# A second attention whose columns and row blocks stand between its transposes, scores and values

## The chip, the cores and the metric

One NeuronCore of a Trainium2 chip runs the whole program. The metric is the device time of one execution in microseconds (us); a kernel has several timed runs, and their median counts. Beside them stands one profiled execution, from which every row below comes. Engines are named as in the profile: PE is TensorE's matmuls, PEld its weight loads, DVE is VectorE, ACT is ScalarE, POOL is GpSimd, SP is the engine that issues the weight DMAs.

## What is computed

Two layers of an encoder over 256 rows of width 1024, in fp32. A layer is a half-weighted FFN, an attention, and another half-weighted FFN, each between two RMS norms:

```python
for i in range(DEPTH):
    g = norm_g[i]
    h = h + FFN_RES * _rmsnorm(_swiglu(_rmsnorm(h, g[0]), ffn1_wg[i], ffn1_wu[i], ffn1_wd[i]), g[1])
    u = _rmsnorm(h, g[2])
    if kind == 0:   m = _diff_attention(u, diff_w_in[j], diff_w_out[j], ...)
    elif kind == 1: m = _neighborhood_attention(u, na_w_in[j], na_w_out[j], na_rpb[j])
    h = h + _rmsnorm(m, g[3])
    h = h + FFN_RES * _rmsnorm(_swiglu(_rmsnorm(h, g[4]), ffn2_wg[i], ffn2_wu[i], ffn2_wd[i]), g[5])
```

The first attention is differential: 8 heads with two key halves of 64 each, two softmaxes of which the second is subtracted with a factor. The second one is a neighbourhood attention: 16 heads of 64, where a row sees a band of 16 columns in all four rows of the grid, with a learned bias.

## The kernel before, in words

All products are made with split operands: a weight or an activation x is written as hi + lo (ACT copies hi, DVE subtracts to get lo), and a product is hi*hi + hi*lo + lo*hi. So each 512 KB piece of weights is loaded by SP (L109), copied by ACT (L134), subtracted by DVE (L135), and then used by TensorE. `Weights.get` asks for splits four pieces ahead and for loads up to eight ahead; four raw buffers and nine split buffers are cycled, and a split buffer is free once both row blocks have used its piece.

There are 256 rows, in two blocks of 128. `proj_rows` makes a 128 x 512 block of one row block (24 products, L402); `proj_cols` makes 256 columns, transposed, for all rows (48 products, L428 to L430); `proj_col` does so for 128 columns of an FFN (16 products, L444 and L446) and leaves two half results, which `gu_cols` adds up: ACT copies one out of the bank (L530), DVE adds the other (L531). `row_steps` makes the down and output products (L469). Banks of TensorE's output memory come in three pools: two for projections ("mm"), four for scores, values and sums ("acc"), two for transposes ("tr").

The second attention (`attn` with key "a1") works on two groups g of eight heads. Of each group there are queries and keys as columns (`qk_cols`, one call for four pairs of heads, in two halves c of 256 columns each; only the first group's queries are made as rows, `qk_rows`, and then transposed, `qk_T`), values as rows (`v_rows`, per row block t). A score step `scores(g, qh, pr)` takes query block qh and four heads pr: 24 short products, biased maxima (L689), exponentials (L698), scalings (L713). The scores of pr = 0 need only the first half of the key columns. `probs_T` transposes the result (L378) and splits it; `av_cols(g, pr)` multiplies with the values (L750) once both query blocks are there, and its result is split into `oT`; `wout` multiplies pieces of `oT` with the output weights, into the sums y0 and y1 of the two row blocks. `queue_bias(1)` queues the loads and the writing of the second group's bias table; they are issued one by one behind weight loads, and `W.extra` issues what is left of them.

The order of the code is a priority, not the order of execution: a planner goes through the program in its own times and gives each engine, among the instructions that it holds to be ready, the one that stands first in the code. `tc.high_priority(offset=n)` counts an instruction as n places earlier; HP2 is 100, and `split_bank` (L362) has it already. Each engine then runs its list in that order, and waits where an operand is late. `hooks` of `proj_rows` call a function behind a given product of a block; what it issues on TensorE may then not come earlier.

Of the kernel before, what the change touches and what calls it, by code (L numbers as in the profile page):

```python
# [155 lines left out]
def encoder_kernel(ctx, tc, x, norm_g, f1g, f1u, f1d, f2g, f2u, f2d,  # L156
# [77 lines left out]
    def bank(pool, tag):  # L234
        return pool.tile([P, 512], F32, tag=tag, name=nm(tag))
# [266 lines left out]
    def ffn(key, li, gains, xg1, xT, last, aside=None):  # L502
# [20 lines left out]
        def gu_cols(p):  # L523
            keys = [[(key, n, p * PW, j) for j in range(KT * PW // UE)] for n in "gu"]
            g = t2p.tile([P, 2, S], F32, tag="t2", name=nm("g"))
            u = t2p.tile([P, 2, S], F32, tag="t2", name=nm("u"))
            for k, y in zip(keys, (g, u)):
                for f in range(2):
                    ps = proj_col(xT, k, f)
                    nc.scalar.activation(y[:, f], ps[:, S:], AF.Copy)  # L530
                    nc.vector.tensor_tensor(out=y[:, f], in0=ps[:, :S], in1=y[:, f], op=ALU.add)  # L531
                if y is g:
                    s = act(flat(g))
            a = gated(flat(u), s)
            ht = l4p.tile([P, 2, 2, S], F32R, tag="l4", name=nm("hT"))
            split_bank(flat(ht[:, 0]), flat(ht[:, 1]), a)
            for f in range(2):
                hT[2 * p + f] = (ht[:, 0, f, :], ht[:, 1, f, :])
# [45 lines left out]
    def attn(key, li, gains, xg1, xT):  # L584
# [8 lines left out]
        def v_rows(g, t):  # L593
            ps = mm_tile()
            proj_rows(ps, xT, t, keys_of(2, g))
# [48 lines left out]
        def qk_cols(part, g):  # L644
            qk_tiles(part, g)
            hi, lo = qk[part, g]
            for c in range(2):
# [164 lines left out]
        else:  # L812
            qk_cols(1, 0)
            qk_T(0, 0, 1)
        if diff:
# [11 lines left out]
        if diff:  # L827
# [8 lines left out]
            probs_T(0, 0, 1)  # L836
            o = av(0, 0)
            qk_rows(1, 1, 0)
# [5 lines left out]
            probs_T(0, 1, 1)  # L844
            o = av(0, 1)
            qk_T(1, 1, 1)
# [31 lines left out]
        W.extra(len(W.extras))  # L878
        scores(0, 0, 0)
        scores(0, 1, 0)  # L880
        qk_cols(0, 1)
# [3 lines left out]
        probs_T(0, 0, 0)  # L885
        probs_T(0, 1, 0)
        qk_cols(1, 1)
        av_cols(0, 0)
        probs_T(0, 0, 1)
        probs_T(0, 1, 1)  # L890
# [4 lines left out]
        v_rows(1, 0)  # L895
        scores(1, 0, 1)
        scores(1, 1, 1)
        gpre, gpost = gains()
        v_rows(1, 1)
        y0 = [mm_tile() for _ in range(2)]  # L900
        probs_T(1, 0, 0)
        probs_T(1, 1, 0)
        wout(y0, 0, [0, 1, 2, 3])
        av_cols(1, 0)
        probs_T(1, 0, 1)
        probs_T(1, 1, 1)
        wout(y0, 0, [4, 5])
        av_cols(1, 1)
        y1 = [bank(ps_acc, "acc") for _ in range(2)]
        wout(y1, 1, [0, 1])  # L910
# [83 lines left out]
```

## Time and profile before

| | us |
|---|---|
| median of 3 runs (1009.20 to 1011.17) | 1010.07 |
| profiled execution, its own time | 1012.26 |
| its span, first to last instruction | 1010.0 |
| TensorE matmul busy | 991.0 |
| DVE busy | 676.2 |
| ACT busy | 588.1 |

The stages lie in the span as follows: first FFN to 201, first attention to 320, then two FFNs to 692, second attention to 818, last FFN. A row of the time-ordered view gives start and length in us, then engine, line, operation, output and inputs by the program's names, shapes, a count, and in square brackets the idle time of the engine before it with what ended that. A matmul row is longer than the time from its start to the next start, since matmuls overlap; pace is read from the starts.

### The profile page before, as it was taken

The page shows a single profiled execution, that of the slowest core. Times are in us where ns is not written, and L with a number is a line of the kernel's source. Part 1 is how long each engine was busy: PE and PEld are TensorE (multiplying, and loading weights), DVE is VectorE, ACT ScalarE, POOL GpSimd, SP SyncE. Part 2 cuts the span into 40 slices and gives each one's busy share as a digit, 9 for nine tenths or more (in the row PEclk, how much of TensorE's full clock was granted, in tenths as well). Part 3 has the DMA queues.
Part 4 walks back from the last instruction along what each step waited for, and adds up shares of the span by engine and source line. Part 5 has one row for each costly group of instructions (what it writes and reads, how often), then busy time and mean ns, then how long its engine had stood idle before and what let it go on. Part 6 is the DMA issues. An engine that isn't in the chain of part 4 may idle for free.

```text
span 1010.0 us, 14628 instructions
## 1 busy us (share of the span) xinstructions
PE 991.0 (98%) x5299; PEld 839.2 (83%) x5299; DVE 676.2 (67%) x1282; ACT 588.1 (58%) x1247; POOL 20.7 (2%) x35
## 2 busy tenths in 40 slices
PE   8999999999999999999999999999999999999997
PEld 4888888888777888888888888888898888888886
DVE  6665656577777656566577576658788687556562
ACT  6655555466777555556456556546675666555551
POOL 0000000000001000000000000000000000000000
PEclk9999999999999999999999999999999999999999
DMA  7767665365533677666367677554735256666631
GB/s 259 237 199 238 186 198 185 115 206 169 197 96 108 204 218 221 204 177 204 94 203 246 194 236 225 191 149 153 240 99 172 84 167 228 190 211 186 203 110 42
DMA packets 121289, 182.83 MB, mean 181 GB/s; under 512 B 6113, under 2 KB 88161, under 8 KB 121218
## 3 DMA queue, kind: packets, MB, share of 16 engines
q1 hardware_dynamic: 121168, 181.78, 57.7%
q8 instruction: 41, 0.67, 0.3%
q14 instruction: 30, 0.25, 0.1%
q0 software_dynamic: 48, 0.13, 0.1%
q10 hardware_dynamic: 2, 0.00, 0.0%
HBM read 180.84 MB, written 1.05 MB: 180 GB/s over the span
## 4 chain that ended last, share of the span: by engine, by line
PE 84%; DMA 5%; DVE 5%; ACT 4%; issue 1%; POOL 0%; SPq 0%; DVEq 0%; POOLq 0%; ACTq 0%
PE acc L469 25%; PE mm L444 24%; PE mm L402 14%; PE mm L446 13%; DVE wlo L135 3%; DMA raw<-in_ffn_wg_dram 2%; PE mm L469 2%; PE tr L378 2%; ACT whi L134 1%; ACT p L698 1%; DMA raw<-in_na_w_in_dram 1%; PE acc L750 1%; PE tr L770 1%; DMA raw<-in_ffn_wd_dram 1%; DMA raw<-in_na_w_out_dram 1%
## 5 line engine op out<-in xcount | busy, mean ns | idle before, releaser
L135 DVE TENSOR_TENSOR wlo<-raw,whi 128x512 fp32r<-128x512 f32 x656 | 421.1, 687 | 194.0 <-ACT whi L134 104.7
L134 ACT ACTIVATE whi<-raw 128x512 fp32r<-128x512 f32 x656 | 366.8, 624 | 169.2 <-PE acc L469 45.8
L444 PE MATMUL mm<-xT,whi 128*128 128x512 f32 x1152 | 288.4, 392 | 2.0 <-DVE g L531 1.9
L444 PEld LDWEIGHTS mm<-xT,whi 128*128 128x128 f32 x1152 | 208.9, 189 | 41.8 <-DVE g L531 3.2
L469 PE MATMUL acc<-whi,hT 128*128 128x512 f32 x704 | 197.0, 391 | 0.0
L402 PE MATMUL mm<-whi,xT 128*128 128x512 f32 x544 | 177.4, 397 | 1.3 <-ACT whi L134 1.1
L446 PEld LDWEIGHTS mm<-xT,wlo 128*128 128x128 f32 x1152 | 157.1, 190 | 11.3
L446 PE MATMUL mm<-xT,wlo 128*128 128x256 f32 x1152 | 160.6, 282 | 0.0
L469 PEld LDWEIGHTS acc<-whi,hT 128*128 128x128 f32 x704 | 130.3, 188 | 25.5
L402 PEld LDWEIGHTS mm<-whi,xT 128*128 128x128 f32 x544 | 102.2, 189 | 22.4 <-ACT whi L134 1.5
L469 PE MATMUL acc<-wlo,hT 128*128 128x512 f32 x352 | 111.2, 390 | 0.0
L402 PE MATMUL mm<-wlo,xT 128*128 128x512 f32 x272 | 108.4, 398 | 0.7 <-DVE wlo L135 0.7
L469 PEld LDWEIGHTS acc<-wlo,hT 128*128 128x128 f32 x352 | 66.1, 188 | 14.1
L402 PEld LDWEIGHTS mm<-wlo,xT 128*128 128x128 f32 x272 | 51.6, 190 | 14.3 <-DVE wlo L135 4.6
L368 ACT ACTIVATE hT<-a 128x512 fp32r<-128x512 f32 x36 | 22.9, 635 | 63.9 <-DVE a L520 63.9
L531 DVE TENSOR_TENSOR u<-mm,u 128x256 f32<-128x256 f32 x72 | 30.4, 422 | 28.0 <-ACT u L530 27.7
L530 ACT ACTIVATE u<-mm 128x256 f32<-128x256 f32 x72 | 26.9, 373 | 29.6 <-PE mm L446 29.6
L530 ACT ACTIVATE g<-mm 128x256 f32<-128x256 f32 x72 | 26.7, 371 | 23.2 <-PE mm L446 23.2
L531 DVE TENSOR_TENSOR g<-mm,g 128x256 f32<-128x256 f32 x72 | 30.3, 421 | 10.2 <-ACT g L530 10.2
L343 DVE TENSOR_TENSOR yg<-acc,gain 128x512 f32<-128x512 f32 x20 | 13.7, 687 | 33.5 <-ACT junk L293 33.4
L293 ACT ACTIVATE junk<-acc 128x512 bf16<-128x512 f32 x20 | 11.8, 591 | 39.2 <-PE acc L469 39.2
L514 ACT ACTIVATE s<-g 128x512 f32<-128x512 f32 x36 | 22.8, 632 | 18.2 <-DVE g L531 18.2
(116 smaller groups left out, 802.3 us busy)
## 6 DMA issues: line engine op xcount, KB each, us to landing
raw<-in_ffn_wg_dram SPq DMA_DIRECT2D x88, 512.0 KB, 4.7
raw<-in_ffn_wu_dram SPq DMA_DIRECT2D x88, 512.0 KB, 4.5
raw<-in_ffn_wd_dram SPq DMA_DIRECT2D x88, 512.0 KB, 4.1
raw<-in_diff_w_in_dram SPq DMA_DIRECT2D x24, 512.0 KB, 4.4
raw<-in_na_w_in_dram SPq DMA_DIRECT2D x24, 512.0 KB, 4.6
gain<-in_norm_g_dram SPq DMA_DIRECT2D x11, 512.0 KB, 5.5
raw<-in_diff_w_out_dram SPq DMA_DIRECT2D x8, 512.0 KB, 4.3
raw<-in_na_w_out_dram SPq DMA_DIRECT2D x8, 512.0 KB, 4.5
```

What stands on the lines that cost most here:

```text
L134: nc.scalar.activation(hi[:, e], raw[:, e], AF.Copy),
L135: nc.vector.tensor_tensor(out=lo[:, e], in0=raw[:, e], in1=hi.bitcast(F32)[:, e], op=ALU.subtract))
L343: nc.vector.tensor_tensor(out=yg[b], in0=ys[b], in1=gpost[:, HALVES[b]], op=ALU.mult)
L368: last_act[0] = nc.scalar.activation(hi, ps, AF.Copy)
L378: nc.tensor.transpose(tr[:, j * P:(j + 1) * P], src[:, j * P:(j + 1) * P], ident)
L402: m = last_pe[0] = nc.tensor.matmul(*a, **k)
L444: nc.tensor.matmul(ps, wh, xT.both(kt), start=kt == 0, stop=False)
L446: nc.tensor.matmul(ps[:, S:], wl, xT.one(0, kt), start=False, stop=kt == KT - 1)
L469: nc.tensor.matmul(ys[b], (xh, xl)[xp](i), parts[i][wp][:, 0, HALVES[b]], start=first and b not in seen, stop=last and left[b] == 0)
L514: nc.scalar.activation(s, g, AF.Silu)
L530: nc.scalar.activation(y[:, f], ps[:, S:], AF.Copy)
L531: nc.vector.tensor_tensor(out=y[:, f], in0=ps[:, :S], in1=y[:, f], op=ALU.add)
```

## The change

In the second attention the calls are put in another order. `qk_cols` takes the halves that it shall make, so that other steps can stand between the two halves: the transposes of the first group's second query block between the halves of its keys; the first half of the second group's queries ahead of the first scores, the second half behind them; the halves of the second group's keys behind one `probs_T` each. `v_rows` takes hooks: the two value row blocks come earlier, and each has a step put behind its eighth product (a `probs_T` in the first, a score step in the second). The output products are taken in smaller portions between transposes. In the first attention a key row block (`qk_rows(1, 1, 0)`) stands ahead of the value product `av(0, 0)`, and the last key transposes stand ahead of `av(0, 1)`. In the FFNs the two instructions that empty a column bank get the priority HP2. No instruction is added or taken away.

```diff
--- before.py
+++ after.py
@@ -527,8 +527,9 @@
             for k, y in zip(keys, (g, u)):
                 for f in range(2):
                     ps = proj_col(xT, k, f)
-                    nc.scalar.activation(y[:, f], ps[:, S:], AF.Copy)
-                    nc.vector.tensor_tensor(out=y[:, f], in0=ps[:, :S], in1=y[:, f], op=ALU.add)
+                    with tc.high_priority(offset=HP2):
+                        nc.scalar.activation(y[:, f], ps[:, S:], AF.Copy)
+                        nc.vector.tensor_tensor(out=y[:, f], in0=ps[:, :S], in1=y[:, f], op=ALU.add)
                 if y is g:
                     s = act(flat(g))
             a = gated(flat(u), s)
@@ -590,9 +591,9 @@
         def keys_of(part, g, c=0, cw=NC):
             return [(key, "i", part * D + g * NC + c, j) for j in range(KT * cw // UE)]
 
-        def v_rows(g, t):
+        def v_rows(g, t, hooks={}):
             ps = mm_tile()
-            proj_rows(ps, xT, t, keys_of(2, g))
+            proj_rows(ps, xT, t, keys_of(2, g), hooks)
             if diff:
                 if t == 0:
                     vv[g] = vp.tile([P, NH, NC], F32, tag="v", name=nm("v"))
@@ -641,10 +642,11 @@
             hi, lo = qk[part, g]
             flip_split(nat.pop((part, g, t)), hi[:, :, q], lo[:, :, q], part == 0)
 
-        def qk_cols(part, g):
-            qk_tiles(part, g)
+        def qk_cols(part, g, pairs=range(2)):
+            if 0 in pairs:
+                qk_tiles(part, g)
             hi, lo = qk[part, g]
-            for c in range(2):
+            for c in pairs:
                 ps = proj_cols(xT, keys_of(part, g, c * PW, PW))
                 j = slice(2 * c, 2 * c + 2)
                 if part == 0:
@@ -810,8 +812,9 @@
             qk_rows(0, 1, 0)
             qk_T(1, 0, 1)
         else:
-            qk_cols(1, 0)
+            qk_cols(1, 0, [0])
             qk_T(0, 0, 1)
+            qk_cols(1, 0, [1])
         if diff:
             lt = t2p.tile([P, NC], F32, tag="t2", name="lam_in")
             nc.gpsimd.dma_start(lt[:, :256], bcast(dlam[0].rearrange("a e -> (a e)"), P))
@@ -834,16 +837,16 @@
             probs_T(0, 0, 0)
             scores(0, 1, 1)
             probs_T(0, 0, 1)
+            qk_rows(1, 1, 0)
             o = av(0, 0)
-            qk_rows(1, 1, 0)
             qk_T(0, 1, 1)
             qk_rows(1, 1, 1)
             qk_T(1, 1, 0)
             o_T(0, 0, o)
             probs_T(0, 1, 0)
             probs_T(0, 1, 1)
+            qk_T(1, 1, 1)
             o = av(0, 1)
-            qk_T(1, 1, 1)
             W.extra(len(W.extras))
             gpre, gpost = gains()
             scores(1, 0, 0)
@@ -876,38 +879,40 @@
             xg = norms(1, y1, gpost, gpre, False)
             return xg, nxT
         W.extra(len(W.extras))
+        qk_cols(0, 1, [0])
         scores(0, 0, 0)
         scores(0, 1, 0)
-        qk_cols(0, 1)
+        qk_cols(0, 1, [1])
         scores(0, 0, 1)
         scores(0, 1, 1)
         queue_bias(1)
         probs_T(0, 0, 0)
+        qk_cols(1, 1, [0])
         probs_T(0, 1, 0)
-        qk_cols(1, 1)
+        qk_cols(1, 1, [1])
         av_cols(0, 0)
         probs_T(0, 0, 1)
-        probs_T(0, 1, 1)
+        v_rows(1, 0, {KT: lambda: probs_T(0, 1, 1)})
         W.extra(len(W.extras))
         scores(1, 0, 0)
         scores(1, 1, 0)
         av_cols(0, 1)
-        v_rows(1, 0)
-        scores(1, 0, 1)
+        v_rows(1, 1, {KT: lambda: scores(1, 0, 1)})
         scores(1, 1, 1)
         gpre, gpost = gains()
-        v_rows(1, 1)
         y0 = [mm_tile() for _ in range(2)]
         probs_T(1, 0, 0)
+        wout(y0, 0, [0, 1])
         probs_T(1, 1, 0)
-        wout(y0, 0, [0, 1, 2, 3])
+        wout(y0, 0, [2, 3])
         av_cols(1, 0)
         probs_T(1, 0, 1)
+        y1 = [bank(ps_acc, "acc") for _ in range(2)]
+        wout(y1, 1, [0])
         probs_T(1, 1, 1)
         wout(y0, 0, [4, 5])
         av_cols(1, 1)
-        y1 = [bank(ps_acc, "acc") for _ in range(2)]
-        wout(y1, 1, [0, 1])
+        wout(y1, 1, [1])
         wout(y0, 0, [6, 7])
         xg = norms(0, y0, gpost, gpre, False)
         wout(y1, 1, [2, 3])
```

## Rows read from the trace of the kernel before

**Rows 1.** The page, part 1: busy time, share and instructions of each engine.

```profile
PE 991.0 (98%) x5299; PEld 839.2 (83%) x5299; DVE 676.2 (67%) x1282; ACT 588.1 (58%) x1247; POOL 20.7 (2%) x35
```

**Rows 2.** Stages: length; busy PE, PEld, DVE, ACT, POOL; clock; DMA share; GB/s.

```profile
90.00:170.00 80.00, 80.00 (x432) 69.26 (x431) 51.30 (x92) 44.15 (x89) 0.00 (x0) 1.00 0.65 202
715.50:745.00 29.50, 28.12 (x225) 26.92 (x223) 21.24 (x55) 19.78 (x45) 0.00 (x0) 0.94 0.57 185
732.70:736.10 3.40, 3.40 (x20) 3.18 (x18) 2.85 (x14) 2.84 (x11) 0.00 (x0) 0.50 0.53 163
745.00:778.00 33.00, 30.96 (x248) 28.20 (x248) 30.15 (x84) 21.84 (x57) 0.00 (x0) 1.00 0.60 187
778.00:810.00 32.00, 30.87 (x191) 26.22 (x191) 22.65 (x57) 18.74 (x45) 0.00 (x0) 1.00 0.23 68
```

**Rows 3.** TensorE by time (start, length, line, tiles, idle before), second attention, beginning.

```profile
715.87 0.28 PE L428 MATMUL mm<-xT,whi 128*128 128x256 f32 x1
...
727.38 0.60 PE L378 MATMUL tr<-ident,nat 128*128 128x128 f32 x4
727.91 0.39 PE L669 MATMUL acc<-qk,qk 64*128 64x256 f32 x2
728.83 0.39 PE L428 MATMUL mm<-xT,whi 128*128 128x256 f32 x1
...
731.30 0.39 PE L669 MATMUL acc<-qk,qk 64*128 64x256 f32 x2 [1.38 <-ACT qk L368]
...
744.93 0.39 PE L669 MATMUL acc<-qk,qk 64*128 64x256 f32 x2
```

**Rows 4.** ACT, then DVE, in order of time in the same part.

```profile
728.54 0.64 ACT L134 ACTIVATE whi<-raw 128x512 fp32r<-128x512 f32 x1 [1.18 <-DMA raw<-in_na_w_in_dram]
...
730.87 0.39 ACT L368 ACTIVATE qk<-tr 128x256 fp32r<-128x256 f32 x1 [0.41 <-DVE qk L369]
...
725.75 2.49 DVE L135 TENSOR_TENSOR wlo<-raw,whi 128x512 fp32r<-128x512 f32 x4
```

**Rows 5.** TensorE in order of time: idle times later in the second attention.

```profile
749.44 0.33 PE L378 MATMUL tr<-ident,p 128*128 128x128 f32 x1 [0.73 <-DVE aT L369]
...
765.97 0.38 PE L669 MATMUL acc<-qk,qk 64*128 64x256 f32 x1 [0.49 <-DVE oT L369]
...
767.41 0.44 PE L378 MATMUL tr<-ident,p 128*128 128x128 f32 x2 [0.83 <-DVE aT L369]
...
788.03 0.50 PE L469 MATMUL mm<-whi,oT 128*128 128x512 f32 x1 [0.82 <-DVE v L369]
```

**Rows 6.** Groups by line: busy us, mean ns, idle before; DVE, transposed banks and biased maxima.

```profile
L369 DVE TENSOR_TENSOR aT<-tr,aT 128x512 fp32r<-128x512 f32 x16 | 10.7, 688 | 1.6 <-ACT aT L368 1.3
...
L689 DVE CUSTOM_DVE_ANT_0 p<-acc,bias 128x256 f32<-128x256 f32 x32 | 11.9, 420 | 0.0
```

**Rows 7.** TensorE in order of time: tail of the second attention.

```profile
809.70 0.39 PE L469 MATMUL acc<-whi,oT 128*128 128x512 f32 x1
...
816.50 1.03 PE L378 MATMUL tr<-ident,xg 128*128 128x128 f32 x8
```

**Rows 8.** TensorE in order of time, first attention.

```profile
253.08 0.47 PE L402 MATMUL mm<-whi,xT 128*128 128x512 f32 x1
...
256.04 1.16 PE L770 MATMUL tr<-v,aT 128*128 128x128 f32 x8 [0.87 <-ACT aT L734]
...
281.37 0.39 PE L669 MATMUL acc<-qk,qk 64*128 64x256 f32 x2 [0.30 <-ACT p L698]
```

**Rows 9.** First column block of the second FFN: TensorE, ACT; who waited for L531.

```profile
350.59 0.50 PE L444 MATMUL mm<-xT,whi 128*128 128x512 f32 x1 [0.92 <-DVE g L531]
...
348.24 1.16 ACT L134 ACTIVATE whi<-raw 128x512 fp32r<-128x512 f32 x2 [1.73 <-DMA raw<-in_ffn_wd_dram]
349.30 0.36 ACT L530 ACTIVATE g<-mm 128x256 f32<-128x256 f32 x1
...
  PE mm L444: 1.9, 4
```

## The prediction

> **What bounds the kernel now.** I read four views in this order. First the engine table of the page: TensorE is busy 98% of the span [rows 1]. Second the stages: in a plain FFN stretch TensorE is busy 80.00 of 80.00 us, while the second attention (715.5 to 810) leaves it idle 1.38, 2.04 and 1.13 us in its three parts [rows 2]. A busy share hides part of the loss here, because matmuls overlap and short ones are counted long, so the third view is the order of TensorE's starts in that attention: the time from one start to the next, against the spacing that the same instruction has when nothing holds it up. The fourth is what ACT and DVE do while TensorE waits.
>
> The reader is to see that the kernel is bound by TensorE nearly everywhere, that no re-ordering gains anything in the FFN's steady part, and that all there is to win lies in the two attentions and at the first column block of each FFN. It is small: by the bounds worked out below 6.6 us in the second attention, 1.5 us in the first one and 1.9 us in the FFNs, out of 1012.26 us.
>
> **Part 1, key and query columns of the second attention.** The first half of a column block needs nothing of the second, and two halves took 727.38 - 715.87 = 11.51 us, so one takes 5.75 us [rows 3]. Before, both halves of the key columns run, then the transposes of the second query block (0.53 us), then its scores. The first score step takes 0.92 us (727.91 to 728.83); the second can't start, because its query is still being split: TensorE idles 1.38 us until ACT has written it [rows 3]. ACT wrote it late because a weight split that waited 1.18 us for its DMA stood ahead in ACT's queue, and the split itself began only at 730.87 [rows 4]. Just behind that idle time the granted clock is 0.50 for 3.4 us (732.70 to 736.10), the lower of its two levels, 1.2 GHz [rows 2]; the engine had run four transposes, scores and a few columns, and had stood still, before it fell. The stretch from 715.87 to the third score step at 744.93 took 29.06 us [rows 3].
>
> After, the transposes stand between the two halves, and the first half of the next query columns stands ahead of the scores. Between transposes and the scores that need them now lie two halves, 11.5 us, against a wait of some 4 us (727.38 to 731.30), so it is covered with 7 us to spare. The work is the same: four halves (23.0), one set of transposes (0.5), two score steps (1.8): 25.4 us. That this is reached needs the weights: the last four splits of column weights, counted from the first split of this attention, end at 728.2 [rows 4], and the last half that needs them starts later than that. 29.06 - 25.4 = 3.7; some changes of shape between steps cost 0.1 to 0.2 each, so **3.4 us** is taken. Bounds: 3.7 if all goes, 2.0 if the clock falls all the same (half of 3.4 us is 1.7).
>
> **Part 2, the rest of the second attention.** The idle times with a named releaser are 0.73 (transposes behind DVE's split of the ones before), 0.49 (scores behind the clearing of value banks), 0.83 (transposes again) and 0.82 us (output product behind the split of a value block) [rows 5], 2.87 in all. Each has one cause: two steps of the same kind stand next to each other, and the second needs a bank that ACT and DVE, one after the other, must first empty. A transposed bank takes DVE 0.688 us [rows 6], behind a copy of much the same length on ACT, while the next transposes come some 0.4 us behind. After, each pair is parted by 5.75 us of columns, by eight products of a row block (1.8 us), by a pair of output blocks (twelve products, 2.7 us, at the 0.23 us that thirty took each from 809.70 to 816.50 [rows 7]) or by a single one (1.4 us). These cover 1.4 us, but a softmax has a long chain too: four biased maxima at 0.420 on DVE, [rows 6], four exponentials on ACT with reads of the sums, four scalings on DVE: I estimate three times the 1.7 us of the maxima, 5 us. The scores that a hook puts inside a value row block have 10 us and more until their transposes, and those inside the first block have been scored some 15 us before. What speaks against full cover is DVE: it is busy 30.15 of 33.00 us from 745 to 778 [rows 2], so its queue is long where three of the four waits lie. I take half, **1.4 us**. Bounds: 2.87 if all of them vanish; a loss of 1.7 if hooks make two new waits like the longest, 0.83. Moved steps issue DMAs as well: the second bias tables and the weights behind them stand on SP in the order of the columns and of the value blocks, and both come earlier or as before; the output weights need parts of the value blocks' buffers, released at the end of the second value block, which also comes earlier. The two gain loads stand behind it, as before.
>
> **The tail of that attention.** From the end of the first row block's products at 809.70 to the transposes of its norm at 816.50 TensorE had 6.8 us of other products [rows 7], which filled the chain of the norm. One of the eight blocks that were cover there (0.23 x 6 = 1.4 us) is now used earlier, between transposes. Products of later blocks can fill its place, and then lack ahead of the norm: I put the cost at nothing up to 1.0 us, inside the bounds above.
>
> **Part 3, first attention.** A key row block moves ahead of the value product. Before, the product stood still 0.87 us for ACT's copy of the transposed probabilities, though some of the 24 row products had been put ahead of it from 253.08 on [rows 8], eight or nine in the 2.1 us that are left. With all 24 ahead there are 16 more at 0.23, 3.6 us, so this goes; two changes between the kinds of work go with it, at some 0.1 each. Who waits for it: the output's transposes, behind another row block (5.5 us), about as long as the chain of four squares, a power on POOL and four scalings; a margin near 1 us stays. The second edit, key transposes ahead of the next value product, gives their split some 1.8 us more; a wait of 0.30 us behind exponentials follows it [rows 8], and whether that moves depends on DVE's order. Together **1.2 us**; bounds 1.5 and, where the margin is missed, -1.0.
>
> **Part 4, column banks first.** All FFN banks of the column form get a priority in the planned order of ACT and DVE. Before, TensorE stood still for such a bank in four places, 1.9 us in all, the one at 350.59 for 0.92 us; there ACT emptied the bank at 349.30, though the next bank's products had long begun, since a weight split that had waited 1.73 us for its DMA was ahead of it [rows 9]. That split is of down weights, by its DMA's name, and the second pair of those is asked for only with the up columns, behind the bank's own evacuation in the code. So the program's order had the bank first already, and the plan, by its own times, put the split ahead; a priority decides between what is ready at one time, and can leave this as it is. In the steady part TensorE waits for nothing [rows 2], so nothing can be gained there, and a weight split put back by one bank (some 0.4 us on either engine) has slack. I take **0**; bounds: a gain of 1.9, a loss of 0.6, one weight split.
>
> **The sum.** 3.4 + 1.4 + 1.2 + 0 = 6.0 us. The profiled execution took 1012.26 us (span 1010.0 and 2.26 around it), so 1006.3 by its clock; it lies 2.2 us above the median of the runs shown, 1010.07, and on that the sum gives 1004.1 us. All bounds at once: 3.7 + 2.9 + 1.5 + 1.9 = 10.0 us less (1000.1), or 2.0 - 1.7 - 1.0 - 0.6 = 1.3 us more (1011.4).
>
> **Rivals.**
> DVE becomes the limit. With part 1 TensorE comes to the third score step 3.4 us earlier, but DVE still has 30.15 us of work where TensorE has 33 [rows 2], and transposes, scores and value products need its output in turn. Then part 2 gives nothing and a third of part 1 comes back as waits: 3.4 - 1.2 + 0.6 of part 3 = 2.8 us, 1007.3. For it: three of the four waits end on DVE. Against: before 745 DVE is idle 8.3 of 29.5 us, and the earlier columns allow weight splits to move there. 0.22.
>
> The change doesn't do what it says. The planned order is by readiness, not by the code: in the trace row products of a step that the code has behind the value product ran ahead of it [rows 8]. If the plan had made the same order already, only the names move: 1010.1, within 0.2%, which is about 2.0 us and what a measurement of this kernel can tell from no change. Against: the query's own products ended where the columns began, at 715.87, and their transposes ran at 727.38 [rows 3], so the code's order does decide between steps that are ready. 0.13.
>
> The FFN's four waits go as well, with most of part 2: 3.6 + 2.3 + 1.3 + 1.6 = 8.8, 1001.3. 0.10.
>
> The clock falls again and again, and the kernel is slower. In the second attention more kinds of short work now follow each other, each with a small pause; one fall costs up to 1.7 us as in 732.70 to 736.10 [rows 2]. It eats the gain from the fourth fall on; six falls would give 1004.1 + 10.2 = 1014.3. Against: the parts from 745 to 810 have idle time of 3.2 us in all, and a clock of 1.00 [rows 2]. 0.07. The Trainium skill ("TensorE: Matmul & The Clock Gate", section "A second HAM failure mode: psum-queue depth-cycling") states that a TensorE which idles briefly and often between groups of matmuls, while it cycles through PSUM banks, can swing between the two clock levels. By that rule the finer alternation would cost what this rival says; the trace shows one such fall, and none in the 65 us behind it that alternate in the same way.
>
> **How the numbers follow.** The forecast has 0.48, with a range of its own from 1002 to 1006.5. Faster by over 0.2%: 0.48 + 0.10 + 0.19 of the DVE rival = 0.77. Within: 0.13 + 0.03 = 0.16. Slower: 0.07. The range leaves out half of the largest gain and the slower case, and takes in the DVE rival and most of no change: 1001.0 to 1009.8.
>
> **What would show it.** Part 1: the four halves, transposes and first two score steps within 25.4 to 26 us, no idle time ahead of a score step there, and a granted clock of 1.00. Part 2: idle time between 745 and 810, in the same steps, about halved; if it stays near 3 us with DVE above 0.9, DVE was the limit. Part 3: no wait ahead of the first value product. Part 4: the waits for L531 still there, four of them. A changed FFN outside its first column block, a granted clock under 0.98 in the attention, or new waits ahead of the hooked transposes and scores would make the prediction wrong.

## The result and the profile after

The changed kernel takes 1002.93 us in the median of 5 runs (1000.87 to 1005.27), against 1011.17 for the kernel before beside it; the ratio is 0.993, with an interval from 0.991 to 0.995. One of the five runs of the kernel before took 1196.89 us and stays out of the ratio. So the changed kernel is faster, by about 0.7%; the forecast was 1004.1. Its profiled execution took 1004.32 us, with a span of 1001.9.

The stages are told apart by the starts of TensorE's instructions, which both traces have. Each stage runs from one such start to the next, so the first FFN takes in the norm and the row blocks up to the first score, and the two FFNs what stands around them. Lengths in us:

| stage | before | after | difference |
|---|---|---|---|
| start to the first FFN column | 38.52 | 39.99 | +1.47 |
| first FFN | 204.50 | 203.93 | -0.57 |
| first attention, first score to first output product | 45.87 | 43.06 | -2.81 |
| from there to the last output product | 31.23 | 31.23 | 0 |
| two FFNs | 395.75 | 395.90 | +0.15 |
| second attention, first key column to third score step | 29.06 | 25.35 | -3.71 |
| third score step to first output product | 41.11 | 39.97 | -1.14 |
| first output product to the end of the first row block's | 23.66 | 22.50 | -1.16 |
| rest of that attention, norm, last FFN | 200.33 | 199.99 | -0.34 |

The second attention gives 6.0 us and the first one 2.8. The start, which the change doesn't touch, differs by 1.5 us; over all the traces of this case it took 37.5 to 40.4, so a whole time can't tell a step of 1 us, and the experiments are read by stages.

The stages of the second attention after, columns as in [rows 2] (length; busy PE, PEld, DVE, ACT, POOL; clock; DMA share; GB/s):

```profile
90.00:170.00 80.00, 80.00 (x431) 69.23 (x430) 51.00 (x90) 44.82 (x90) 0.00 (x0) 1.00 0.66 203
713.70:739.40 25.70, 25.70 (x223) 25.29 (x221) 20.25 (x47) 18.19 (x40) 0.00 (x0) 1.00 0.76 240
739.40:773.00 33.60, 32.18 (x260) 29.25 (x259) 29.64 (x88) 22.30 (x57) 0.00 (x0) 1.00 0.46 141
773.00:802.20 29.20, 28.97 (x182) 24.54 (x183) 23.81 (x61) 19.61 (x50) 0.00 (x0) 1.00 0.37 115
```

The steady FFN is as it was. The first part of the attention has no idle time any more and a clock of 1.00 throughout, where [rows 2] show 1.38 us idle and the lower level for 3.4 us. The last part lost nearly all of its idle time. The middle part kept 1.42 us, and there DVE is busy 29.64 of 33.60.

TensorE in order of time, answering to [rows 3]:

```profile
714.11 0.28 PE L428 MATMUL mm<-xT,whi 128*128 128x256 f32 x1
...
719.87 0.60 PE L378 MATMUL tr<-ident,nat 128*128 128x128 f32 x4
720.22 0.36 PE L428 MATMUL mm<-xT,whi 128*128 128x256 f32 x1
...
731.90 0.39 PE L671 MATMUL acc<-qk,qk 64*128 64x256 f32 x2
...
739.47 0.39 PE L671 MATMUL acc<-qk,qk 64*128 64x256 f32 x2
```

One half of the keys (5.76 us), the transposes, another half, half of the next queries, and then two score steps with nothing between them and no bracket. (A score step has twelve products on TensorE in both traces, not the 24 that the description of the kernel gives it.)

The waits that the middle of that attention has instead of those in [rows 5], TensorE again, and then ACT and DVE ahead of the first of them:

```profile
761.47 1.25 PE L378 MATMUL tr<-ident,p 128*128 128x128 f32 x8 [0.79 <-DVE aT L369]
...
767.57 0.30 PE L752 MATMUL acc<-aT,v 128*64 128x256 f32 x1 [0.24 <-DVE mx L691]
768.26 1.00 PE L752 MATMUL acc<-aT,v 128*64 128x256 f32 x7 [0.39 <-DVE mx L691]
```

```profile
757.63 1.15 ACT L134 ACTIVATE whi<-raw 128x512 fp32r<-128x512 f32 x2 [1.92 <-DMA raw<-in_na_w_out_dram]
758.69 1.19 ACT L368 ACTIVATE oT<-acc 64x512 fp32r<-64x512 f32 x2
759.91 1.08 ACT L368 ACTIVATE aT<-tr 128x512 fp32r<-128x512 f32 x2
```

```profile
756.75 2.49 DVE L135 TENSOR_TENSOR wlo<-raw,whi 128x512 fp32r<-128x512 f32 x4
```

The bracket at 761.47 names DVE, but ACT stood still 1.92 us for the DMA of a weight, split two pieces of it, and only then copied the value banks and the transposed banks that DVE and TensorE waited for. DVE was not free either until 759.24: it made the subtractions of four split pieces. It is the picture of [rows 9] in another stage, and of [rows 4].

The first attention after, answering to [rows 8]; the second row has the value product's transposes, now without a wait, the third the two score steps that before were parted, the fourth the one that waited:

```profile
253.98 0.47 PE L402 MATMUL mm<-whi,xT 128*128 128x512 f32 x1
...
259.55 1.95 PE L772 MATMUL tr<-v,aT 128*128 128x128 f32 x16
...
273.80 0.39 PE L671 MATMUL acc<-qk,qk 64*128 64x256 f32 x2
...
279.49 0.39 PE L671 MATMUL acc<-qk,qk 64*128 64x256 f32 x2
```

### The profile page after: what moved, and what is told of

It is laid out like the page before. It is cut to its first block, busy times and chain, and to the rows that moved or that the text cites. A ratio compares the mean times of both kernels' runs of the same rounds, so it can differ in the third digit from the quotient of the medians.

```text
span 1001.9 us, 14629 instructions
## 1 busy us (share of the span) xinstructions
PE 987.5 (99%) x5299; PEld 838.6 (84%) x5299; DVE 674.8 (67%) x1282; ACT 586.5 (59%) x1247; POOL 20.8 (2%) x35
## 4 chain that ended last, share of the span: by engine, by line
PE 90%; DVE 6%; ACT 2%; DMA 1%; issue 1%; POOL 0%; DVEq 0%; POOLq 0%; ACTq 0%
PE mm L444 26%; PE acc L469 25%; PE mm L402 17%; PE mm L446 13%; PE tr L378 2%; DVE wlo L135 2%; PE mm L469 2%; PE tr L772 1%; DVE p L691 1%; DVE aT L369 1%; ACT whi L134 1%; DVE p L715 1%; PE mm L428 1%; DMA raw<-in_ffn_wg_dram 1%; PE mm L430 1%
## 5 line engine op out<-in xcount | busy, mean ns | idle before, releaser
L469 PEld LDWEIGHTS acc<-whi,hT 128*128 128x128 f32 x704 | 130.4, 188 | 25.4
L531 ACT ACTIVATE u<-mm 128x256 f32<-128x256 f32 x72 | 26.9, 373 | 29.7 <-PE mm L446 29.7
L531 ACT ACTIVATE g<-mm 128x256 f32<-128x256 f32 x72 | 26.7, 371 | 23.4 <-PE mm L446 23.4
```

The costliest lines, as they stand in the source:

```text
L469: nc.tensor.matmul(ys[b], (xh, xl)[xp](i), parts[i][wp][:, 0, HALVES[b]], start=first and b not in seen, stop=last and left[b] == 0)
```

## Experiments

The letters of stages: "A" is the first attention from its first score to its first output product, "K" the second one from the first key column to the third score step, "M" from there to the first output product, "O" from there to the end of the first row block's output products. Before: A 45.87, K 29.06, M 41.11, O 23.66. After: 43.06, 25.35, 39.97, 22.50.

**Part 1 alone.** The kernel before with the halves of columns (and the argument of `qk_cols` for them):

```diff
-            qk_cols(1, 0)
+            qk_cols(1, 0, [0])
             qk_T(0, 0, 1)
+            qk_cols(1, 0, [1])
...
+        qk_cols(0, 1, [0])
         scores(0, 0, 0)
         scores(0, 1, 0)
-        qk_cols(0, 1)
+        qk_cols(0, 1, [1])
```

> The kernel before with part 1 alone: key columns of the second attention in halves with the query's transposes between them, and the first half of the next query columns ahead of the first scores. Theory (the 1.38 us wait and what follows it were the loss): the stretch from the first key column to the third score step shrinks from 29.06 us to 25.4, no wait ahead of a score step in it, granted clock 1.00; the rest of the second attention keeps its waits (2.87 us in four places), so the whole gains 3.5 to 4 us. Rival (DVE is the limit behind it): the stretch shrinks as far, but the part behind it, 744.93 to 809.70 = 64.8 us before, grows by 1.2 us or more. Rival (nothing but the order of names changes): 29 us again.

Measured: 1007.27 us, ratio 0.997 (0.996 to 0.998). K 25.36, M 40.23, O 23.66, A unchanged.

**The transposes alone.** Only the first four lines of that diff; the query halves stay together behind the scores:

> The kernel before with one edit: the query's transposes between the two halves of the key columns; the next query columns stay whole and behind the first two score steps. Theory (the clock fell for the wait): the second score step finds its query split, the wait of 1.38 us is gone, and with it the stretch at a granted clock of 0.50, so the same stretch takes about 25.5 to 26 us, nearly the whole gain of part 1. Rival (the clock falls for the alternation of short scores and columns, not for the wait): no wait, but again some 3.4 us at 0.50, and about 27 us.

Measured: 1007.08 us, ratio 0.996 (0.995 to 0.998). K 25.36, M 40.32, O 23.66. Its stretch of K (length, busy times, clock as above):

```profile
716.60:742.00 25.40, 25.40 (x223) 24.98 (x221) 21.04 (x55) 19.33 (x44) 0.00 (x0) 1.00 0.66 215
```

So the transposes between the key halves bring the whole 3.7 us; one half of columns (5.75 us) covers the wait, and the query half ahead of the scores adds nothing that these stages show (89.25 and 89.34 us in K, M and O). M is 0.8 to 0.9 us shorter as well, though no step in it moved. How much of that follows from the edit stays open: in the two kernels below, which leave the second attention as it was, M is 40.56 and 41.25, so it varies by some 0.7 us by itself: of its waits in [rows 5] the one ahead of the scores, 0.49 us there, is gone in the first and 0.64 in the second.

**The first attention alone**, and of it **the key transposes alone.** The kernel before with

```diff
+            qk_rows(1, 1, 0)
             o = av(0, 0)
-            qk_rows(1, 1, 0)
...
+            qk_T(1, 1, 1)
             o = av(0, 1)
-            qk_T(1, 1, 1)
```

and with the second pair of lines only:

> The kernel before with part 3 alone, both edits of the first attention. Theory: from the first row products behind the second transposes (253.08 before) to the first output products of that attention (288.88) 35.8 us become 33.9 as in the changed kernel, and nothing else moves: 1.9 us faster. Rival (the gain seen in the changed kernel came from the priority of column banks, by another state of DMA and splits at the start of that attention): 35 us or more here.

> The kernel before with only the second edit of the first attention: the last key transposes ahead of the second value product. Theory: scores find their keys split, and the waits from 275.30 to 281.37 (one of 0.30 us behind exponentials, and two short ones) go: 0.7 us. Rival (this edit does nothing, all 1.9 us come from the key row block that moved): under 0.2 us in that stretch.

Measured: both 1007.97 us, ratio 0.998 (0.997 to 1.000), A 43.05. The key transposes alone 1010.83 in one run, A 44.27. So they give 1.6 us, and the key rows 1.2 (by difference); A tells this well, being 45.82 to 45.87 in the three traces with neither edit and 43.03 to 43.07 in the nine with both. Both runs gave more than was expected of them, 2.8 for 1.9 and 1.6 for 0.7. (The stretch that was to become 33.9 as in the changed kernel is 33.0 there, 253.98 to 286.98.)

What the key rows give is the wait of [rows 8] at 256.04 and a change of work or two, as the prediction had it. What the key transposes give is not the small thing it was taken for. In the kernel before, the two score steps of the second group took from 275.30 to 277.55, with a row product among them, and the third from 280.45 to 282.27, of which the 0.30 in [rows 8] is only the recorded part. After, they take 273.80 to 275.43 and 279.49 to 280.41. Before, the keys came late, and the scores began 1.2 us later than with the key transposes alone moved, counted from the first score of the attention. DVE then took other work ahead of the maxima that the exponentials need; ACT stood still 3.28 us for these, the exponentials began 3.3 us later, and the third score step waited for banks that they read. Scores and exponentials before, then the exponentials with the key transposes alone moved:

```profile
275.30 0.50 PE L669 MATMUL acc<-qk,qk 64*128 64x256 f32 x4
275.74 0.49 PE L402 MATMUL mm<-whi,xT 128*128 128x512 f32 x1
...
279.38 0.47 ACT L698 ACTIVATE p<-acc,nmx 128x256 f32<-128x256 f32 x1 [3.28 <-DVE nmx L682]
```

```profile
275.73 0.47 ACT L698 ACTIVATE p<-acc,nmx 128x256 f32<-128x256 f32 x1
```

These two kernels also left the second attention as it was, and so bear on when the clock falls. Its wait ahead of the second score step, in the first kernel and in the second:

```profile
726.83 0.39 PE L669 MATMUL acc<-qk,qk 64*128 64x256 f32 x2 [1.06 <-ACT qk L368]
```

```profile
730.03 0.39 PE L669 MATMUL acc<-qk,qk 64*128 64x256 f32 x2 [1.66 <-ACT qk L368]
```

and the stretches around it, in the same order:

```profile
711.70:741.00 29.30, 28.24 (x249) 27.05 (x248) 22.83 (x57) 20.99 (x47) 0.00 (x0) 1.00 0.62 197
```

```profile
714.30:743.70 29.40, 27.74 (x223) 26.59 (x221) 20.87 (x54) 19.34 (x45) 0.00 (x0) 0.94 0.55 181
731.20:734.60 3.40, 3.40 (x20) 3.18 (x20) 2.86 (x16) 2.69 (x12) 0.00 (x0) 0.50 0.47 135
```

Behind 1.06 us idle the clock stays at 1.00 and K is 27.27; behind 1.66, as behind the 1.38 of [rows 3], it is 0.50 for 3.4 us, and K is 29.34 (29.06). The three traces have the same instructions there in the same order, so the fall went with the longer wait, whose size varies from run to run; in the ten traces without that wait K is 25.35 to 25.36 and the clock 1.00. But the length alone doesn't decide. Among the plain columns of the second FFN, TensorE stood still 1.42 us in the changed kernel and 1.64 us in the first of these two, and the clock stayed at 1.00 in both:

```profile
352.15 1.66 PE L444 MATMUL mm<-xT,whi 128*128 128x512 f32 x6 [1.42 <-DVE g L532]
```

```profile
350.02 2.14 PE L444 MATMUL mm<-xT,whi 128*128 128x512 f32 x8 [1.64 <-DVE g L531]
```

What sets the two cases apart was not tried. By the three traces, 1.5 to 1.7 us of part 1's 3.7 hang on it (the difference of K less that of the waits, and half of 3.4).

**Without the priority of the column banks.** The changed kernel less part 4:

```diff
-                    with tc.high_priority(offset=HP2):
-                        nc.scalar.activation(y[:, f], ps[:, S:], AF.Copy)
-                        nc.vector.tensor_tensor(out=y[:, f], in0=ps[:, :S], in1=y[:, f], op=ALU.add)
+                    nc.scalar.activation(y[:, f], ps[:, S:], AF.Copy)
+                    nc.vector.tensor_tensor(out=y[:, f], in0=ps[:, :S], in1=y[:, f], op=ALU.add)
```

> The changed kernel without the priority of the column banks (part 4 undone). Theory (the priority changes no engine's order): the same time as the changed kernel, 1003 us within 1.5, and the same waits at the first column blocks of the FFNs, some 1.8 us in all. Rival (the priority helped, and the longer wait of 1.58 us at 350.45 is chance): 2 us or more slower than the changed kernel.

Measured: 1002.86 us, ratio 0.993 (0.991 to 0.995), the changed kernel's own. Each engine has the same instructions in the same order in both, so the priority changes nothing at all. The waits for the banks of first column blocks are there with and without it, and vary from trace to trace. By the starts they are 0.43, 1.08, 0.47 and 0.59 us in the four FFNs before, 1.58 and 0.49 in two of them in the changed kernel, 0.54 and 0.39 without the priority. Who waited for the gate's tile g (us, times) in the latter two:

```profile
  PEld mm L444: 2.5, 4
  PE mm L444: 1.8, 2
```

```profile
  PEld mm L444: 1.3, 3
  PE mm L444: 0.6, 2
```

**The splits held behind the bank.** Since a priority doesn't order them, in the changed kernel the splits that are asked for with the up columns of a first column block are issued on ACT behind the evacuation of the gate's second bank:

```diff
             for k, y in zip(keys, (g, u)):
+                if p == 2 and y is u:
+                    with tc.issue_after(emptied.ins):
+                        for kk in k:
+                            W.get(kk)
                 for f in range(2):
                     ps = proj_col(xT, k, f)
                     with tc.high_priority(offset=HP2):
-                        nc.scalar.activation(y[:, f], ps[:, S:], AF.Copy)
+                        emptied = nc.scalar.activation(y[:, f], ps[:, S:], AF.Copy)
```

> The changed kernel, with one order forced in the first column block of each FFN: the weight splits that are asked for with the up columns stand behind the gate columns' second bank on ACT. Theory (it is the order on ACT that makes TensorE wait for a bank, a split that stands still for its DMA in front of the bank's evacuation): the waits of matmuls L444 for L532, some 1.8 us, vanish, and the kernel is 1.5 to 2.2 us faster than the changed one. Rival (the weights then come too late and TensorE waits for them instead): the waits for L532 go, but waits for L135 of like size come, and the time stays.

Measured: 1000.51 us, ratio 0.991 (0.989 to 0.993). ACT at the second FFN's first block, in the changed kernel and then in this one:

```profile
348.39 1.15 ACT L134 ACTIVATE whi<-raw 128x512 fp32r<-128x512 f32 x2 [1.65 <-DMA raw<-in_ffn_wg_dram]
349.80 1.15 ACT L134 ACTIVATE whi<-raw 128x512 fp32r<-128x512 f32 x2 [0.25 <-PE mm L444]
350.86 0.36 ACT L531 ACTIVATE g<-mm 128x256 f32<-128x256 f32 x1
```

```profile
345.23 0.38 ACT L535 ACTIVATE g<-mm 128x256 f32<-128x256 f32 x1 [2.41 <-PE mm L446]
345.51 1.14 ACT L134 ACTIVATE whi<-raw 128x512 fp32r<-128x512 f32 x2
```

Now ACT waits for TensorE's last product and empties the bank at once; TensorE waits for no such bank in the whole trace. The FFNs are 2.1 us (the two) and 0.3 and 0.6 us (first and last) shorter than in the changed kernel. By the medians the step is 2.4 us. The transposes in the second attention waited 1.10 us in this kernel, M being 40.25; so that wait varies like the others. (M is 39.85 to 40.25 in the three traces with the changed order of that attention and nothing else moved in it.)

**No scaling of probabilities.** The changed kernel, which here leaves out the division of the second attention's probabilities by their sums:

```diff
-                for c in range(2):
-                    for j in range(2):
-                        nc.vector.tensor_scalar(out=ps[c][:, j, :], in0=ps[c][:, j, :],
-                                                scalar1=rz[:, c, j:j + 1], scalar2=None, op0=ALU.mult)
+                pass
```

> The changed kernel, with the scaling of the probabilities by their sums left out in the second attention: 32 instructions on DVE, 9.1 us of its work there, most of it between 741 and 790. Theory (the waits that are left come from banks emptied behind a weight split that stands still for its DMA, and from the order of steps): the wait ahead of the hooked transposes (0.79 us at 761.47) and the two ahead of the value product (0.24 and 0.39 us near 768) stay within 0.3 us of their sizes. Rival (DVE's load is the limit, 29.6 of 33.6 us busy): they vanish, and the second attention is 1.2 us shorter or more.

Measured: M 38.99, O 22.44, one run at 999.62. The wait for transposed probabilities is gone, those of the value product aren't:

```profile
763.11 0.30 PE L749 MATMUL acc<-aT,v 128*64 128x256 f32 x1 [0.24 <-DVE mx L691]
763.80 2.80 PE L749 MATMUL acc<-aT,v 128*64 128x256 f32 x23 [0.39 <-DVE mx L691]
```

That looks like DVE's load, but with less work on DVE the weights were split earlier too: ACT's splits ahead of these transposes ran at 750.25, 39.7 us behind the first key column in place of 43.5, and none stood just ahead of the copies. So it doesn't tell the two causes apart, and the next one was made for that.

**The splits held behind the transposed banks.** The changed kernel; DVE has the same work, though not in the same order, as a piece's subtraction follows its split:

```diff
+        for kk in keys_of(2, 1)[:2]:
+            W.get(kk)
+        with tc.issue_after(last_act[0].ins):
+            for kk in keys_of(2, 1)[2:]:
+                W.get(kk)
         v_rows(1, 0, {KT: lambda: probs_T(0, 1, 1)})
```

> The changed kernel; the splits of the weights for the last two pieces of the second attention's second value block are issued on ACT behind the second evacuation of the transposed probabilities just before it, instead of ahead of it. VectorE's work and its order stay. Theory (order on ACT): in the changed kernel PE waited 0.79 us at 761.47 for the transposed probabilities, and the chain behind it goes over ACT's weight split at 757.63, which had waited 1.92 us for its DMA at the head of ACT's queue. With the split behind the evacuation this wait falls to 0.3 us or less, and the stretch from the third score step to the first output product goes from 39.97 us to about 39.2. Rival (VectorE's load): VectorE carries 29.6 us in that stretch of 33.6 and its copies are what comes last; the wait stays at 0.6 us or more, and the stretch at 39.8 to 40.1. The whole time would be 0.8 us below the changed kernel's by the theory, which the start's own scatter of 1.4 us hides; the stretch decides.

Measured: M 39.01, 1002.04 in one run. TensorE has no wait there, and ACT copies ahead of the splits:

```profile
759.00 0.66 PE L378 MATMUL tr<-ident,p 128*128 128x128 f32 x4
759.42 0.48 PE L402 MATMUL mm<-whi,xT 128*128 128x512 f32 x1
759.74 0.60 PE L378 MATMUL tr<-ident,p 128*128 128x128 f32 x4
```

```profile
757.43 1.09 ACT L368 ACTIVATE aT<-tr 128x512 fp32r<-128x512 f32 x2
758.40 1.15 ACT L134 ACTIVATE whi<-raw 128x512 fp32r<-128x512 f32 x2
```

The split now begins 45.3 us behind the first key column, later than its DMA had landed in the changed kernel (757.63 is 43.5 us behind it), so no engine stands still for it. So splits ahead of the copies are what made this wait; the fastest kernel below, which has the same edit, shows M at 39.00 again. But the edit took them out of both engines' way. In the changed kernel four subtractions kept DVE until 759.24, and the first copy on ACT, behind its split, was ready at 759.27; here DVE had nothing before its first copy and stood still for ACT:

```profile
756.83 1.40 DVE L369 TENSOR_TENSOR oT<-acc,oT 64x512 fp32r<-64x512 f32 x2 [1.60 <-ACT oT L368]
```

So the share of the order on ACT and that of DVE's queue aren't told apart.

**Hooks later.** The changed kernel with the hooked transposes at the 16th product, the value product `av_cols(0, 1)` inside the second value block behind its 8th product, and the score step behind the 16th:

```diff
-        v_rows(1, 0, {KT: lambda: probs_T(0, 1, 1)})
+        v_rows(1, 0, {2 * KT: lambda: probs_T(0, 1, 1)})
...
-        av_cols(0, 1)
-        v_rows(1, 1, {KT: lambda: scores(1, 0, 1)})
+        v_rows(1, 1, {KT: lambda: av_cols(0, 1), 2 * KT: lambda: scores(1, 0, 1)})
```

> The changed kernel with the transposes in the first value row block behind its 16th product in place of the eighth, and the value product that waits for banks put behind the eighth product of the second value row block. Theory (both waits are a matter of cover, 0.8 and 0.63 us): both vanish, and the second attention from its first key column (714.11) to the end of the first row block's output products (801.94) takes 86.4 us in place of 87.8. Rival (the cover is taken from later steps): new waits of like size ahead of the transposes behind it, and 87.5 us or more.

Measured: M 37.99, O 23.42, 1000.07 in one run. K, M and O together are 86.8 us, between the theory's 86.4 and the rival's 87.5. All three waits of the middle are gone, 2.0 us, and 0.9 comes back ahead of the second pair of output products, with DVE's order in front of it:

```profile
775.61 0.50 PE L469 MATMUL mm<-whi,oT 128*128 128x512 f32 x1 [0.86 <-DVE v L369]
```

```profile
773.66 1.29 DVE L135 TENSOR_TENSOR wlo<-raw,whi 128x512 fp32r<-128x512 f32 x2
774.87 0.68 DVE L369 TENSOR_TENSOR v<-mm,v 128x512 fp32r<-128x512 f32 x1
```

**All orders together.** The changed kernel with the two held orders above, the output weights' splits held behind the second value block in the same way, and in the first attention an output block between the last transposes:

```diff
+            wout(y1, 1, [2])
             probs_T(1, 1, 1)
...
-            wout(y1, 1, [2, 3])
+            wout(y1, 1, [3])
```

Once as that, and once with the value product hooked into the second value block besides:

> The changed kernel with the same kind of edit at four places: the splits asked for beside the first column block of each FFN behind its gate's second bank on ACT (as measured alone), those of the second value block behind the transposed probabilities, those of the output weights behind the value block, and in the first attention one output weight block asked for between the last two transposes of probabilities instead of before both. Theory (a split that waits for its DMA at the head of ACT's queue is what is left to gain): the FFNs give 2 to 3 us, the transposed probabilities 0.8, the first attention's 0.98 us wait at 299.46 goes; about 999 us against the changed kernel's 1002.9, a ratio of 0.989 to 0.990 to the kernel before. Rival (the waits are VectorE's): only the FFNs' share comes, about 1000.5, ratio 0.9906, and the waits at 299 and 761 stay within 0.2 us of their size.

> As the run with the four edits, and the second attention's first value product of the second query half is issued inside the second value block (after 8 of its products) rather than ahead of it, with the score step after 16. Theory: the value product's waits of 0.24 and 0.39 us go as well, since its key rows have 8 products more to be copied; about 0.6 us less than the four edits, 998.4, ratio 0.989. Rival: the later value block evacuates later, and a wait ahead of the output products takes their place, as the 0.86 us one at 775.61 did where the same move stood alone; then the time is that of the four edits or up to 0.3 us more.

Measured: 998.37 us, ratio 0.989 (0.987 to 0.990), and 998.68, ratio 0.989 (0.987 to 0.991). The first is the fastest here, faster than the changed kernel by 4.6 us between the medians, of which the stages carry 3.3: FFNs 2.2, first attention 0.4 (its two waits near the end, 0.98 and 0.81 us by the starts, became three of 0.55, 0.36 and 0.44), second attention 0.7. The start lies 1.7 us lower in its trace besides, and goes with no edit. The hook took 0.8 us from M (38.22 against 39.00) and gave 1.2 back in O (24.01 against 22.80), so its rival was right. One late bank is left in the FFNs, in the fastest kernel at another FFN's first block, where another split waits for its DMA on ACT:

```profile
553.40 1.89 PE L444 MATMUL mm<-xT,whi 128*128 128x512 f32 x7 [0.99 <-DVE g L536]
```

```profile
551.05 1.15 ACT L134 ACTIVATE whi<-raw 128x512 fp32r<-128x512 f32 x2 [1.47 <-DMA raw<-in_ffn_wu_dram]
552.11 0.37 ACT L535 ACTIVATE g<-mm 128x256 f32<-128x256 f32 x1
```

## Why the prediction was right, point by point

**Bound.** That TensorE sets the time, and that only the attentions and first column blocks have anything to give, held: the stages outside the attentions moved by 0.6 us or less but for the start.

**Part 1**: forecast 3.4, measured 3.7, its upper bound; the sum of the parts (four halves, transposes, two score steps: 25.4) was the measured length to 0.05 us. The 0.1 to 0.2 set aside for changes between kinds of work weren't additional, as the pieces' own lengths held them. The clock, which the bound of 2.0 allowed for, didn't fall. What did it was one edit, not two: the transposes.

**Part 2**: forecast 1.4, measured 1.4 (the 6.0 us of K, M and O less the 4.6 that part 1 gives alone), and up to 0.9 more, if the 0.9 that M fell with part 1 alone is only its own scatter. Part 2 was not run by itself. By place it was otherwise than forecast: the middle gave 0.3 and the output products, parted by transposes, 1.2 (O is 23.64 to 23.66 in the five traces without that edit, 22.44 to 22.50 in the five with it and nothing else moved there). Of this, 0.30 us stood in no term: the list of waits lacks a fifth one, though the idle time in [rows 2] has it (2.04 and 1.13 are 3.17, not 2.87); it is gone after:

```profile
797.68 0.72 PE L469 MATMUL mm<-whi,oT 128*128 128x512 f32 x2 [0.30 <-ACT oT L368]
```

In the middle, the 0.83 of [rows 5] stayed: it is the 0.79 at 761.47, ahead of the transposes that are hooked now. A wait there was one of the prediction's own signs of being wrong, and the eight products of a row block that were to cover it were not enough while splits stood ahead of the copies. The reason put against full cover was DVE's queue. The waits that came (0.79, 0.24, 0.39, 0.23) do name DVE, but the largest went when splits were put behind the copies, on ACT and with them on DVE; so DVE's queue may have had a part in it, and is not shown to be the cause. The 0.24 and 0.39 at the value product wait for biased maxima on DVE; they kept these sizes with 32 instructions less on DVE, and only moving that product took them away. The rival in which DVE becomes the limit saw where waits would come; its price, all of part 2 and a third of part 1, did not come.

**The tail**: nothing was lost. From the end of the first row block's products to the norm's transposes it is 801.94 to 808.75, 6.8 us as in [rows 7], in these rows:

```profile
801.94 0.62 PE L469 MATMUL acc<-whi,oT 128*128 128x512 f32 x2
...
808.75 1.03 PE L378 MATMUL tr<-ident,xg 128*128 128x128 f32 x8
```

**Part 3**: forecast 1.2, measured 2.8, over its bound of 1.5; this is the term that was mis-sized. The key row block was right (1.2 for 0.87 and some 0.2). The key transposes were put at next to nothing, because only the recorded wait of 0.30 was looked at; they were 1.6, since three score steps that ran with gaps and other products between them came together. The clue stood in the view used elsewhere, the spacing of starts.

**Part 4**: forecast 0, measured 0, since every engine's order is the same with and without the priority. That the plan held the split to be ready first fits this, but the plan's own times are on no row. The sign had four waits left; there were two, of 1.8 us in all. What is to be won there was more than the bound of 1.9: held back by an order on ACT, the splits gave 2.4 us in the FFNs against the kernel without the priority, and 3.0 against the changed one.

**The rival in which the clock falls again and again** had nothing for it: in the 88 us of the changed attention the clock is 1.00. The rule of the Trainium skill ("TensorE: Matmul & The Clock Gate", section "A second HAM failure mode: psum-queue depth-cycling") that was weighed there did not come to bear: waits of up to 0.79 us between groups of products, in all of the finer alternation, brought no fall; in the kernels with the old order of this attention a single one of 1.38 or 1.66 did, while 1.42 and 1.64 in plain columns did not.

**The sum**: 6.0 forecast. By stages it was 8.8 in the two attentions; with the start's +1.5 and the FFNs' -0.8 the span is 8.1 us shorter. The medians differ by 7.1 us from the 1010.07 shown and by 8.2 from that of the runs beside it. What the forecast lacked is 1.6 in part 3, 0.3 in part 1 and 0.9 in M, of which only the first is a term that was mis-sized. That the median lies within 1.2 us of the forecast is in part luck: the scatter of the start, and of the median that the sum is taken from (1010.07 or 1011.17), is about as large as what the forecast lacked, and in the profiled pair the longer start took back 1.5 us of it.

## What to carry to other kernels

Where one engine's list holds both splits that wait for a DMA and the evacuation of banks, look for a split with "<-DMA" just ahead of a late evacuation; the bracket names the last engine of the chain, here DVE, while holding back the split, with the work on DVE that follows it, took the wait away. An order between the two instructions helped where a priority did not. Put one block of products between transposes and what reads them: here 5.75 us of columns were enough for a wait of some 4 us, and a second block added nothing. Price a moved step by the spacing of starts over the whole stretch to the next fixed step, not by the idle time that has a bracket.

## What was not expected

At one place of the second attention, with the same instructions around it, the granted clock stayed at 1.00 behind 1.06 us idle and was 0.50 for 3.4 us behind 1.38 and 1.66. Waits of 1.42 and 1.64 us in plain columns left it at 1.00, so the length of the wait is not all. And the start of the program, up to the first FFN column, took 37.5 to 40.4 us in kernels that are equal there, by where the clock fell: 37.5 to 38.2 in the five traces with a fall at 7.6 to 8.3, 39.5 to 40.4 in the five with one at 22.9 to 24.3, 38.0 to 38.5 in the three with none. So only the later fall goes with a longer start. That alone moves the whole time by as much as most of the steps above; why it falls in one place or the other was not tried.
